# Hybrid decoder layer: block loads moved to another queue, sums and head pairs reordered

## The chip, the cores and the metric

One core of one Trainium2 chip runs the whole layer in one launch. The metric is device time in microseconds, the median of several runs. The kernel before takes 1122.39 us (median of 3 runs, 1122.03 to 1122.48).

## What is computed

One layer on a sequence of 256 tokens with a model width of 2048, all in float32: one input projection, two token mixers side by side (chunked gated linear attention with 4 heads, and differential attention with 16 heads), two branch projections merged by sigmoid gates, an output projection, and a residual sum.

```python
h = rmsnorm(x, pre_norm_g[l])
proj = h @ w_in[l]
(a_q, a_k, a_v, a_g, a_lr, b_q, b_k, b_v, b_g, m_a, m_b) = jnp.split(proj, offsets, axis=-1)
gk = jax.nn.log_sigmoid((a_lr @ gla_gk_w2[l] + gla_gk_b[l]).astype(jnp.float32)) / GATE_LOGIT_NORMALIZER
o_a = gla_chunked(a_q, a_k, a_v, gk)             # reshaped to 4 heads
o_a = rmsnorm(o_a, gla_norm_g[l]).reshape(B, S, GLA_VAL_DIM) * jax.nn.silu(a_g)
y_a = o_a @ w_branch_a[l]
o_b = diff_attention(b_q, b_k, b_v, lam)         # 16 heads, two softmaxes each
o_b = rmsnorm(o_b, diff_norm_g[l]) * (1.0 - lam_init)
o_b = o_b.reshape(B, S, DIFF_VAL_DIM) * jax.nn.silu(b_g)
y_b = o_b @ w_branch_b[l]
merged = jax.nn.sigmoid(m_a) * y_a + jax.nn.sigmoid(m_b) * y_b
x = x + rmsnorm(merged @ w_out[l], post_norm_g[l])
```

## The kernel before, in words

**Products in float32.** Each weight tile is split into a rounded half `hi` (ScalarE, line 244) and a rest `lo` (VectorE, line 245), and TensorE takes three products of the halves of both operands. A weight tile arrives as `raw` (SyncE's queue, line 216) and is split by halves: `emit_half` makes one half ready, up to `AHEAD` = 4 halves before it is used; `raw`, `hi` and `lo` have 3 buffers each. `half_tile` (line 413) uses one half in 12 matmuls of up to 512 columns; `token_major` (line 424) does the 8 halves of 512 output columns; `channel_major` (line 446) does 128 output channels, transposed, in two halves of 8 matmuls of 512 and 8 of 256 columns.

**Four stretches.** First the value columns `v0`, `v2`, `v3` (to about 81 us). Then the *sets* (to about 447 us): five groups of columns computed as 2 x 2 blocks with seven products instead of eight, `PRODUCTS` = (1, 3, 5, 6, 2, 7, 4), each product in four steps (`t`, `h`), 28 steps a set and 140 in all. `phase_steps` (line 77) mixes 64 half tiles of other columns (`others`, line 621) between them. Then the gates of the linear attention (`ag0` to `ag3`), the merge gates and the heads' channel tiles, with both mixers' attention as background tasks. At the end the branch projections `y0` (lines 1035 to 1045) and `y1`, and the output projection.

**A set's blocks.** Four tiles in 4 buffers (`chain`): `a` and `b` for t = 0, 1, loaded whole by `link` (line 171, 1 MB each, SyncE's queue). Products 1 and 5 and 6 and 4 use `a`, products 3 and 7 use `b`, product 2 uses plain tiles `c` (line 189). `follow_set` (line 195) lets GpSimd's queue add a third block to `a` behind product 1 and to `b` behind product 6 (an accumulating transfer of 1 MB, line 201); VectorE adds `b` to `a` ahead of the splits of product 6 (line 192) and `c` to `a` behind those of product 2 (line 199). Products 1, 6, 7 and 4 share one PSUM bank `x`; VectorE reads it between product 7 and product 4 (line 724).

**Background tasks.** `pump(n)` (line 381) lets each of the first n tasks issue its next segment (up to its next `yield`) behind the half tile just issued. `token_major` pumps after every second half tile, `channel_major` is followed by one `pump(2)`. The tasks are `forget_gate` (line 470), `gla_scores` (line 750), `gla_out` (line 838) for both halves of the linear attention's heads, and one `diff_pair` (line 907) for each two heads of the differential attention: fetch of query and key tiles that had been spilled to memory, split into `q2`, `kh`, `kl` (`diff_split`, line 894), and for each head four segments (scores and exponentials; combination; transposes; values, norm and gate), and a last one that transposes and writes `obh`, `obl` (line 984). `settle` (line 1059) finishes every task before the last two half tiles of the first `y1` tile. `token_major` takes two of the four `mm` banks, the tasks use the four `bg` banks.

**Order.** `ag0`-`ag3`, `m01`, heads 0 and 1, `m02`, a loop that pumps until both halves of the linear attention are out (line 1032), `y0`, heads 2 and 3, `m03`, `y1`, output. Group 0's channel tiles are made in the sets' stretch (`EARLY`); for groups 0 to 2 (`STORED`) query and key are spilled, for group 3 they are split at once. For group 3 the values `dv3` and gates `bg3` are made in `diff_heads`.

**Buffers.** Tag `u`: 18 tiles of 4 KB a partition. Tag `u2`: `MORE` = 13 tiles of 4 KB, for the linear attention's temporaries, its result `oah`, `oal` (8 tiles, read by `y0`), `obh`, `obl` (2 for each group, read by `y1`), and group 3's values and gates. Within the tile framework an instruction waits until a buffer of its tile's tag is free; the order of instructions on an engine is the framework's, by the order of the program and its own estimate of what is ready.

Of the kernel before, what the change touches and what calls it, by code (L numbers as in the profile page):

```python
# [14 lines left out]
P = 128  # L15
D = 2048
S = 256
# [12 lines left out]
LEAD = 6  # L30
EARLY = (0,)
STORED = (0, 1, 2)
# [44 lines left out]
def phase_steps():  # L77

    keys = ["v4"] + [f"{name}{hf}{c}" for hf in range(2) for name in ("k", "q") for c in range(4)]
    keys += [f"{name}{g}{c}" for g in EARLY for pair in range(2) for name in ("dq", "dk") for c in (2 * pair, 2 * pair + 1)]  # L80
    keys += ["m00"]
    other = [(key, r, h) for key in keys for r in range(4 if key in ("v4", "m00") else 1) for h in range(2)]
    steps = [("set", s, prod, t, h) for s in range(SETS) for prod in PRODUCTS for t in range(2) for h in range(2)]
    mixed = []
# [7 lines left out]
def hybrid_kernel(ctx: ExitStack, tc, xt, xn, preg, postg, w, w2, gkb, glag, lamv, diffg, ident_d, causal_d, lmask_d, out):  # L92
# [66 lines left out]
    seq += halves_of(*(f"ag{g}" for g in range(4)), "m01") + heads_order(0) + heads_order(1) + halves_of("m02")  # L159
    seq += halves_of(*(f"y0{g}" for g in range(4))) + heads_order(2) + heads_order(3) + halves_of("m03")  # L160
# [10 lines left out]
    def link(s, name, t):  # L171
        count[0] += 1
        c = blocks.tile([P, 2048], F32, tag="chain", name=f"{name}_{count[0]}", bufs=4)
        sp.dma_start(c, weights(f"set{s}", {"a": 0, "b": 6}[name] + t)[0])
        chain[s, name, t] = c

    def emit_set(s, prod, t, h):
        c = slice(1024 * h, 1024 * h + 1024)
        if h == 0 and prod == 1:
            if s == 0:  # L180
                link(s, "a", t)
            link(s, "b", t)
        if h == 0 and prod == 4 and s + 1 < SETS:
            link(s + 1, "a", t)
        n = 4 * PRODUCTS.index(prod) + 2 * t + h + LEAD - 4 * PRODUCTS.index(2)
        if 0 <= n < 4:
            i, j = n // 2, n % 2
            raws[s, i, j] = u([P, 1024], "c")
            sp.dma_start(raws[s, i, j], weights(f"set{s}", 4 + i)[0][:, 1024 * j : 1024 * j + 1024])
        a, b = chain[s, "a", t], chain[s, "b", t]  # L190
        if prod == 6:
            dve.tensor_tensor(out=a[:, c], in0=a[:, c], in1=b[:, c], op=ALU.add)
        return raws[s, t, h] if prod == 2 else (b if prod in (3, 7) else a)[:, c]

    def follow_set(s, prod, t, h):
        c = slice(1024 * h, 1024 * h + 1024)
        a, b = chain[s, "a", t], chain[s, "b", t]
        if prod == 2:
            dve.tensor_tensor(out=a[:, c], in0=a[:, c], in1=raws[s, t, h], op=ALU.add)
        if h == 1 and prod in (1, 6):  # L200
            pool.dma_start(a if prod == 1 else b, weights(f"set{s}", 2 + t)[0], accum_op=ALU.add)

    def emit_plain(j, key, r, h):
# [6 lines left out]
        early = key == "v0"  # L210
        if h == 0:
# [234 lines left out]
    def channel_major(key):  # L446
        o = ps("mm")
        for h in range(2):
            half_channel(o, h, *take(key))
        return o[:, :S], o[:, S:]  # L450
# [19 lines left out]
    def forget_gate():  # L470
# [10 lines left out]
        w2_raw, w2_s = u([P, 1024], "w2_raw"), u([P, 1024], "w2_s", F32R)  # L481
        pool.memset(w2_raw, 0.0)
        for i in range(4):
            pool.dma_start(w2_raw[32 * i : 32 * i + RANK, :], w2)
        yield
# [120 lines left out]
    gspill = [None] * (2 * SETS)  # L606
    ts, heads, m0 = {}, {}, []
# [13 lines left out]
    def others():  # L621
# [24 lines left out]
        for g in EARLY:  # L646
            for pair in range(2):
                for name in ("dq", "dk"):
                    t = t2([P, 2, S], name)
                    for c in range(2):  # L650
                        o = ps("bg")
                        for h in range(2):
# [5 lines left out]
                            yield  # L658
        banks = [ps("bg"), ps("bg")]
# [90 lines left out]
    def gla_scores(hf):  # L750
# [22 lines left out]
        for n, m in enumerate(LEVELS):  # L773
# [10 lines left out]
            if m == 1:  # L784
                pool.tensor_tensor(out=xqv, in0=xqv, in1=view(k, 0, *early), op=ALU.mult)
# [44 lines left out]
        yield  # L830
# [7 lines left out]
    def gla_out(hf, gates):  # L838
# [27 lines left out]
        for j in range(4):  # L866
# [8 lines left out]
            if j % 2:  # L875
# [16 lines left out]
    parts = {}  # L892

    def diff_split(g, pair, tq, tk):
        q2, kh, kl = parts[g, pair] = [u([P, 2, 2, S], name, F32R) for name in ("q2", "kh", "kl")]
        for m in range(2):
            own, other = slice(64 * m, 64 * m + 64), slice(64 - 64 * m, P - 64 * m)
            act.activation(q2[own, m], tq[own], AF.Copy)
            dve.tensor_tensor(out=q2[other, m], in0=tq[own], in1=f32(q2[own, m]), op=ALU.subtract)
            act.activation(kh[own, m], tk[own], AF.Copy)  # L900
            act.activation(kh[other, m], tk[own], AF.Copy)
            dve.tensor_tensor(out=kl[own, m], in0=tk[own], in1=f32(kh[own, m]), op=ALU.subtract)
            pool.memset(f32(kl[other, m]), 0.0)
        done.add(f"split{g}{pair}")
        yield

    def diff_pair(g, pair, values):
# [7 lines left out]
        if g in STORED:  # L915
            tq, tk = (fetch(heads[g, pair, name], name, lambda shape, name, dtype: t2(shape, name)) for name in ("dq", "dk"))
            yield
            yield from diff_split(g, pair, tq, tk)
        while f"split{g}{pair}" not in done:
            yield  # L920
        q2, kh, kl = parts[g, pair]
        vv, uu = values
        for h in (2 * pair, 2 * pair + 1):
# [53 lines left out]
            yield  # L977
# [8 lines left out]
        yield  # L986

    def diff_heads(g):
# [14 lines left out]
        for pair in range(2):  # L1003
            made = []
            for name in () if g in EARLY else ("dq", "dk"):
# [4 lines left out]
                if g in STORED:  # L1010
                    heads[g, pair, name] = spill(t, name)
                else:
                    made.append(t)
            if made:
                tasks.insert(0, diff_split(g, pair, *made))
# [12 lines left out]
    diff_heads(0)  # L1028
    diff_heads(1)
    merge_gate(token_major("m02", 512, x_ops, 2))  # L1030

# [14 lines left out]

    diff_heads(2)
    diff_heads(3)
# [169 lines left out]
```

## Time and profile before

| | before |
|---|---|
| runs, median (lowest to highest) | 1122.39 us (1122.03 to 1122.48) |
| the profiled execution's own time | 1123.6 us |
| its span, first to last instruction | 1121.8 us |
| granted TensorE clock, mean | 0.997 |
| TensorE matmuls busy | 1105.6 us, 5570 matmuls |
| VectorE, ScalarE, GpSimd busy | 831.8, 677.1, 111.8 us |
| memory traffic | 257.76 MB, mean 230 GB/s |

The profile's page gives busy time of each engine and the costliest groups of instructions. In a row of a group the first number behind the bar is its busy time, the second the mean duration of one in ns, the third the idle time of its engine ahead of it. The view of waits has, for each waiting engine and line and each engine that released it, the sum in us, how often, and the longest. PE is TensorE, DVE VectorE, ACT ScalarE, POOL GpSimd, SP SyncE; a `q` behind them means their sequencer. Matmuls overlap: a matmul's duration is longer than the distance to the next one's start.

### The profile page before, as it was taken

To read this page: it belongs to the slowest core of one execution; us is meant where nothing else is said; L and a number is where in the kernel's file an instruction comes from. 1 tells how busy PE (TensorE), PEld (TensorE's weight loads), DVE (VectorE), ACT (ScalarE), POOL (GpSimd) and SP (SyncE) were. 2 spreads that over 40 slices of the span, in tenths; PEclk is the share of its full clock that TensorE was granted. 3 is DMA by queue.
4 is the path that set the end of the run, shared out by engine and by line. 5 is a ranking of instruction groups with operands and counts; after the bars stand their busy time and mean duration, and the time that the engine had idled before them with its cause. 6 is when DMAs were issued, how large, how long until landed. Compare 5 with 4: busy or idle time off the path is not lost. (4 is left out here: it accounts for less than half of the span.)

```text
span 1121.8 us, 15070 instructions
## 1 busy us (share of the span) xinstructions
PE 1105.6 (99%) x5570; PEld 945.4 (84%) x5570; DVE 831.8 (74%) x1160; ACT 677.1 (60%) x997; POOL 111.8 (10%) x165
## 2 busy tenths in 40 slices
PE   9999999999999999999999999999999999999996
PEld 7998888888888888878888888788888888788886
DVE  7878979779789798699965866766676766655463
ACT  7856666666666666765655755655675665444450
POOL 0101010000100100340021202111200010000000
PEclk9999999999999999999999999999999999999998
DMA  8799797696996973945586567565645474556752
GB/s 313 261 412 243 260 321 221 221 304 188 336 254 218 313 210 123 317 167 185 174 291 243 200 220 257 202 228 176 237 165 184 158 308 161 180 188 218 269 188 75
DMA packets 46042, 257.76 MB, mean 230 GB/s; under 512 B 5841, under 2 KB 7377, under 8 KB 23441
## 3 DMA queue, kind: packets, MB, share of 16 engines
q1 hardware_dynamic: 31968, 198.59, 49.4%
q0 software_dynamic: 12992, 56.89, 18.1%
q10 hardware_dynamic: 1008, 1.32, 0.4%
q8 instruction: 43, 0.70, 0.2%
q14 instruction: 31, 0.25, 0.1%
HBM read 236.86 MB, written 19.92 MB: 229 GB/s over the span
## 5 line engine op out<-in xcount | busy, mean ns | idle before, releaser
L245 DVE TENSOR_TENSOR lo<-raw,hi 128x1024 fp32r<-128x1024 f32 (+3 forms) x307 | 369.1, 1205 | 183.8 <-ACT hi L244 180.8
L244 ACT ACTIVATE hi<-raw 128x1024 fp32r<-128x1024 f32 (+3 forms) x307 | 315.8, 1032 | 282.0 <-PE mm L421 144.6
L421 PE MATMUL mm<-hi,xs 128*128 128x512 f32 (+1 forms) x704 | 171.4, 385 | 0.0
L421 PEld LDWEIGHTS mm<-hi,xs 128*128 128x128 f32 x704 | 130.2, 188 | 21.2
L245 DVE TENSOR_TENSOR lo<-a,hi 128x1024 fp32r<-128x1024 f32 x80 | 97.2, 1221 | 19.0 <-ACT hi L244 18.0
L244 ACT ACTIVATE hi<-a 128x1024 fp32r<-128x1024 f32 x80 | 84.7, 1059 | 39.4 <-PE mm L706 20.0
L441 PE MATMUL mm<-xs,hi 128*128 128x512 f32 x384 | 100.5, 396 | 0.0
L441 PE MATMUL bg<-xs,hi 128*128 128x512 f32 x384 | 99.5, 390 | 0.2 <-ACT hi L244 0.2
L421 PE MATMUL mm<-lo,xs 128*128 128x512 f32 (+1 forms) x352 | 91.9, 383 | 0.7 <-DVE lo L245 0.7
L441 PEld LDWEIGHTS bg<-xs,hi 128*128 128x128 f32 x384 | 72.1, 188 | 14.7 <-ACT hi L244 0.6
L441 PEld LDWEIGHTS mm<-xs,hi 128*128 128x128 f32 x384 | 69.2, 189 | 11.8
L421 PEld LDWEIGHTS mm<-lo,xs 128*128 128x128 f32 x352 | 65.8, 188 | 12.9 <-DVE lo L245 1.6
L706 PE MATMUL mm<-hi,xs 128*128 128x512 f32 x240 | 65.1, 393 | 0.8 <-DVE gr L724 0.8
L443 PEld LDWEIGHTS bg<-xs,lo 128*128 128x128 f32 x384 | 52.3, 190 | 4.9 <-DVE lo L245 1.2
L443 PEld LDWEIGHTS mm<-xs,lo 128*128 128x128 f32 x384 | 52.4, 190 | 3.8
L245 DVE TENSOR_TENSOR lo<-b,hi 128x1024 fp32r<-128x1024 f32 x40 | 48.6, 1221 | 8.5 <-ACT hi L244 7.8
L443 PE MATMUL bg<-xs,lo 128*128 128x256 f32 x384 | 53.6, 282 | 0.8 <-DVE lo L245 0.8
L443 PE MATMUL mm<-xs,lo 128*128 128x256 f32 x384 | 53.5, 282 | 0.0
L706 PEld LDWEIGHTS mm<-hi,xs 128*128 128x128 f32 x240 | 44.4, 188 | 9.7 <-DVE gr L724 1.5
L421 PE MATMUL mm<-hi,oah 128*128 128x512 f32 x128 | 50.7, 396 | 0.0
L421 PE MATMUL mm<-hi,obh 128*128 128x512 f32 x128 | 50.7, 399 | 0.0
L421 PE MATMUL mm<-hi,obl 128*128 128x512 f32 x128 | 50.1, 392 | 0.0
(301 smaller groups left out, 1966.6 us busy)
## 6 DMA issues: line engine op xcount, KB each, us to landing
raw<-in_w_dram SPq DMA_DIRECT2D x136, 1024.0 KB, 5.0
raw<-in_w_dram SPq DMA_DIRECT2D x14, 832.0 KB, 6.0
a<-in_w_dram SPq DMA_DIRECT2D x10, 1024.0 KB, 6.3
b<-in_w_dram SPq DMA_DIRECT2D x10, 1024.0 KB, 7.4
c<-in_w_dram SPq DMA_DIRECT2D x20, 512.0 KB, 10.3
a<-in_w_dram POOLq DMA_DIRECT2D x10, 1024.0 KB, 15.1
b<-in_w_dram POOLq DMA_DIRECT2D x10, 1024.0 KB, 9.5
raw<-in_w_dram SPq DMA_DIRECT2D x4, 800.0 KB, 9.7
```

The costliest lines, as they stand in the source:

```text
L244: act.activation(hi_t[:, a:b], r[:, a:b], AF.Copy)
L245: dve.tensor_tensor(out=lo_t[:, a:b], in0=r[:, a:b], in1=f32(hi_t[:, a:b]), op=ALU.subtract)
L421: i = pe.matmul(banks[b][:, :n], a[part][:, P * b : P * b + P], w[:, n * j : n * j + n], start=first, stop=last)
L441: i = pe.matmul(o, hi[:, c], x_pair(kt), start=kt == 0, stop=kt == KT - 1)
L443: i = pe.matmul(o[:, :S], lo[:, c], x_ops(kt)[0], start=False, stop=False)
L706: i = pe.matmul(out, a[part], w[:, 512 * j : 512 * j + 512], start=first, stop=last, skip_group_check=out is x)
```

## The change

The five parts:

1. In the sets, `link` loads go to GpSimd's queue from the second set on and are issued about two steps earlier each (set 0's two `a` blocks with the first half of `v3`); the accumulating transfers go by halves of a tile; the sums `a+b` and `a+c` stand behind the splits of earlier steps.
2. `phase_steps` puts four other half tiles behind the first four steps and spreads the remaining 60 evenly.
3. `gla_scores` multiplies and adds on VectorE what GpSimd did; `w2_raw` is filled during the sets, and `forget_gate` loses its first `yield`.
4. Every pair's query and key are spilled and fetched twice, once on each half of the partitions, so that the split is done on all 128 partitions at once.
5. All heads' channel tiles come ahead of `y0`; a task whose head 0 is done is pumped also at the half tiles between pumps (`pump_eager`); closing `yield`s are dropped; `settle` is called behind the first half tile of `y1`.

```diff
+FRONT = 4
...
-        mixed += other[len(other) * i // len(steps) : len(other) * (i + 1) // len(steps)]
+        due = min(i + 1, FRONT) + (len(other) - FRONT) * (i + 1) // len(steps)
+        mixed += other[put:due]
+        put = due
...
-    seq += halves_of(*(f"ag{g}" for g in range(4)), "m01") + heads_order(0) + heads_order(1) + halves_of("m02")
-    seq += halves_of(*(f"y0{g}" for g in range(4))) + heads_order(2) + heads_order(3) + halves_of("m03")
+    seq += halves_of(*(f"ag{g}" for g in range(4)), "m01") + heads_order(0) + heads_order(1) + heads_order(2)
+    seq += halves_of("m02") + heads_order(3) + halves_of(*(f"y0{g}" for g in range(4)), "m03")
...
-        sp.dma_start(c, weights(f"set{s}", {"a": 0, "b": 6}[name] + t)[0])
+        (pool if s else sp).dma_start(c, weights(f"set{s}", {"a": 0, "b": 6}[name] + t)[0])
...
-        if h == 0 and prod == 1:
-            if s == 0:
-                link(s, "a", t)
-            link(s, "b", t)
-        if h == 0 and prod == 4 and s + 1 < SETS:
-            link(s + 1, "a", t)
+        if h == 0 and s + 1 < SETS and (prod, t) in ((7, 1), (4, 0)):
+            link(s + 1, "a", 1 - t)
+        if h == 0 and s + 1 < SETS and (prod, t) == (4, 1):
+            link(s + 1, "b", 0)
+        if h == 0 and prod == 1 and (s == 0 or t == 0):
+            link(s, "b", t if s == 0 else 1)
...
-        if prod == 6:
-            dve.tensor_tensor(out=a[:, c], in0=a[:, c], in1=b[:, c], op=ALU.add)
...
-        if prod == 2:
-            dve.tensor_tensor(out=a[:, c], in0=a[:, c], in1=raws[s, t, h], op=ALU.add)
-        if h == 1 and prod in (1, 6):
-            pool.dma_start(a if prod == 1 else b, weights(f"set{s}", 2 + t)[0], accum_op=ALU.add)
+        def accumulate(name, i):
+            pool.dma_start(chain[s, name, i][:, c], weights(f"set{s}", 2 + i)[0][:, c], accum_op=ALU.add)
+
+        if prod == 1:
+            accumulate("a", t)
+        i = {(5, 1): 0, (6, 0): 1, (2, 1): 0, (7, 0): 1}.get((prod, t))
+        if i is not None:
+            a = chain[s, "a", i][:, c]
+            second = prod in (5, 6)
+            dve.tensor_tensor(out=a, in0=a, in1=chain[s, "b", i][:, c] if second else raws[s, i, h], op=ALU.add)
+            if second:
+                accumulate("b", i)
...
+    eager = set()
+
+    def advance(some):
+        with tc.issue_after(latest[0]):
+            for task in some:
+                r = next(task, DONE)
+                (eager.add if r == "go" else eager.discard)(task)
+                if r is DONE:
+                    tasks.remove(task)
+
     def pump(n=1):
-        with tc.issue_after(latest[0]):
-            for task in tasks[:n]:
-                if next(task, DONE) is DONE:
-                    tasks.remove(task)
+        advance(tasks[:n])
+
+    def pump_eager():
+        advance([task for task in tasks[:2] if task in eager])
...
-            if q == 6 and settle:
+            if q == 1 and settle:
                 settle()
             half_tile(banks, n, q, ops, *take(key))
             if q % 2 or "gate" not in done:
                 pump(step)
+            else:
+                pump_eager()
...
-            pool.tensor_tensor(out=dst, in0=src[:, :, 0, :], in1=src[:, :, 1, :], op=ALU.add)
-        pool.tensor_tensor(out=suf, in0=q, in1=k, op=ALU.mult)
+            dve.tensor_tensor(out=dst, in0=src[:, :, 0, :], in1=src[:, :, 1, :], op=ALU.add)
+        dve.tensor_tensor(out=suf, in0=q, in1=k, op=ALU.mult)
...
-                pool.tensor_tensor(out=xqv, in0=xqv, in1=view(k, 0, *early), op=ALU.mult)
+                dve.tensor_tensor(out=xqv, in0=xqv, in1=view(k, 0, *early), op=ALU.mult)
...
+    def twice(t, d):
+
+        for h in range(2):
+            rows = slice(64 * h, 64 * h + 64)
+            pool.dma_start(f32(t[rows]), d.rearrange("(m p) i t -> p m i t", m=2))
...
+        raw = u([P, 2, 2, S], "dq")
+        q2, kh, kl = (u([P, 2, 2, S], name, F32R) for name in ("q2", "kh", "kl"))
+        twice(raw, heads[g, pair, "dq"])
+        twice(kl, heads[g, pair, "dk"])
+        yield
+        act.activation(q2, raw, AF.Copy)
+        act.activation(kh, f32(kl), AF.Copy)
+        for m in range(2):
+            other = slice(64 - 64 * m, P - 64 * m)
+            dve.tensor_tensor(out=q2[other, m], in0=raw[other, m], in1=f32(q2[other, m]), op=ALU.subtract)
+        dve.tensor_tensor(out=kl, in0=f32(kl), in1=f32(kh), op=ALU.subtract)
+        yield
...
-            yield
+            yield "go" if h % 2 == 0 else None
...
-    diff_heads(0)
-    diff_heads(1)
+    for g in range(3):
+        diff_heads(g)
     merge_gate(token_major("m02", 512, x_ops, 2))
+    diff_heads(3)
```

More of the change, by code (lines that the diff above doesn't have):

```diff
@@ L30 @@
 LEAD = 6
+FRONT = 4
 EARLY = (0,)
-STORED = (0, 1, 2)
 BIG = 18
@@ L83, in phase_steps @@
     steps = [("set", s, prod, t, h) for s in range(SETS) for prod in PRODUCTS for t in range(2) for h in range(2)]
-    mixed = []
+    mixed, put = [], 0
     for i, step in enumerate(steps):
         mixed.append(step)
-        mixed += other[len(other) * i // len(steps) : len(other) * (i + 1) // len(steps)]
+        due = min(i + 1, FRONT) + (len(other) - FRONT) * (i + 1) // len(steps)
+        mixed += other[put:due]
+        put = due
     return mixed
@@ L210, in emit_plain @@
         early = key == "v0"
+        if key == "v3" and r == 0 and h == 0:
+            for i in range(2):
+                link(0, "a", i)
         if h == 0:
@@ L449, in channel_major @@
             half_channel(o, h, *take(key))
+            if h == 0:
+                pump_eager()
         return o[:, :S], o[:, S:]
@@ L480, in forget_gate @@
             dve.tensor_tensor(out=lrt[r, :], in0=bank[r, :S], in1=f32(top[r, :S]), op=ALU.subtract)
[L481 to L484, printed above, removed]
-        yield
+        w2_s = u([P, 1024], "w2_s", F32R)
         top = u([P, 1024], "w2h", F32R)
@@ L606, in hybrid_kernel @@
     gspill = [None] * (2 * SETS)
+    w2_raw = u([P, 1024], "w2_raw")
     ts, heads, m0 = {}, {}, []
@@ L658, in others @@
                             yield
+        pool.memset(w2_raw, 0.0)
+        for i in range(4):
+            pool.dma_start(w2_raw[32 * i : 32 * i + RANK, :], w2)
         banks = [ps("bg"), ps("bg")]
@@ L829, in gla_scores @@
         done.add(f"scores{hf}")
-        yield
     for hf in range(2):
@@ L874, in gla_out @@
             split_out(bank, hi, lo, glag_s[:, j : j + 1])
-            if j % 2:
+            if j == 1:
                 yield
@@ L890, in hybrid_kernel @@
     obh, obl = [], []
[L892 to L905, printed above, removed]
+    def twice(t, d):
+        for h in range(2):
+            rows = slice(64 * h, 64 * h + 64)
+            pool.dma_start(f32(t[rows]), d.rearrange("(m p) i t -> p m i t", m=2))
     def diff_pair(g, pair, values):
@@ L914, in diff_pair @@
             values.extend(fetch(gspill[2 * g + 4 + i], name, u) for i, name in enumerate(("dv", "ub")))
[L915 to L921, printed above, removed]
+        raw = u([P, 2, 2, S], "dq")
[10 more added lines that the diff above has]
+        yield
         vv, uu = values
@@ L976, in diff_pair @@
                 dve.scalar_tensor_tensor(out=og[:, h % 2, b, :], in0=bank[:, P * b : P * b + P], scalar=e[:, b : b + 1], in1=uu[:, b, hv], op0=ALU.mult, op1=ALU.mult)
-            yield
+            yield "go" if h % 2 == 0 else None
         bank = ps("bg")
@@ L985, in diff_pair @@
         done.add(f"pair{g}{pair}")
-        yield
     def diff_heads(g):
@@ L1009, in diff_heads @@
                     pump(2)
[L1010 to L1015, printed above, removed]
+                heads[g, pair, name] = spill(t, name)
             tasks.append(diff_pair(g, pair, values))
```

4 lines of the change are left out of this document (removed).

## The prediction

> **What bounds the kernel now.** I read the page first, then TensorE's waits, then the stretches, then the moments of the single waits.
>
> ```profile
> span 1121.8 us, 15070 instructions
> PE 1105.6 (99%) x5570; PEld 945.4 (84%) x5570; DVE 831.8 (74%) x1160; ACT 677.1 (60%) x997; POOL 111.8 (10%) x165
> ...
> PE bg L321 <- DVE ones_b L318: 1.6, 1, 1.6
> PE bg L981 <- DVE ogb L976: 1.5, 2, 0.9
> PE bg L443 <- DVE lo L245: 0.8, 1, 0.8
> PE mm L706 <- DVE gr L724: 0.8, 2, 0.5
> PE mm L421 <- DVE lo L245: 0.7, 2, 0.5
> PE bg L404 <- ACT hi L244: 0.7, 1, 0.7
> PE bg L955 <- DVE prob L951: 0.3, 1, 0.3
> PE bg L441 <- ACT hi L244: 0.2, 1, 0.2
> ```
>
> TensorE works 99% of the span, and the change removes no matmul and adds none. So all it can win is in these waits, and the view lists only 6.6 us of them. L321 and L404 (2.3 us) are the start, which the change doesn't touch; 4.3 us in 9 waits are left. A wait costs more than its idle time, because matmuls overlap:
>
> ```profile
> L421 PE MATMUL mm<-hi,xs 128*128 128x512 f32 x576 | 144.5, 392 | 0.0
> ...
> 712.13 16.34 PE mm L421 x72
> ```
>
> The chain has 72 matmuls in 16.34 us, 0.227 us from start to start, while one lasts 0.392 us. At a wait the overlap of 0.165 us is lost too. The 9 waits are worth 4.3 + 9 x 0.165 = **5.8 us**, 0.5% of the span. That is the ceiling; every new wait comes off it. Everything else the change does (it touches the work of VectorE, ScalarE, GpSimd and the transfers) costs nothing unless it makes TensorE wait.
>
> **The change part by part.** *The sets.* The one wait for `lo` at L443 and what VectorE did before it:
>
> ```profile
> 253.46 2.36 DVE L192 TENSOR_TENSOR a<-a,b 128x1024 f32<-128x1024 f32 x2
> 255.74 1.22 DVE L245 TENSOR_TENSOR lo<-raw,hi 128x1024 fp32r<-128x1024 f32 x1
> ...
> 257.01 1.21 PE L443 MATMUL bg<-xs,lo 128*128 128x256 f32 x8 [0.81 <-DVE lo L245]
> ```
>
> Two sums of product 6 run back to back, 2.36 us, ahead of a `lo` that TensorE needs next. In the new code a sum stands behind a split two or more set steps before its result is used, and ScalarE's `hi` no longer waits for it. There are still four sums in four steps, so the density stays; what goes is that they stand in front of the splits. I take this wait as gone: 0.8 + 0.165 = **0.97**.
>
> The two waits for `gr` (VectorE must read bank `x` before product 4 writes it):
>
> ```profile
> 139.87 0.42 DVE L642 TENSOR_TENSOR k<-k,rstd_bc 128x256 f32<-128x256 f32 x1
> 140.20 0.68 DVE L724 TENSOR_TENSOR gr<-mm,p 128x512 f32<-128x512 f32 x1
> ...
> 140.94 1.19 PE L706 MATMUL mm<-hi,xs 128*128 128x512 f32 x4 [0.51 <-DVE gr L724]
> ```
>
> The read stood behind the finish of a key channel, 0.42 us. I counted the mix: of 64 half tiles on 140 steps none is put behind step 23 (the last of product 7) in the first three sets. With 4 in front and 60 on 140, 12 a set, one stands there in every set, and it is the second half of a channel, whose finish then comes after `gr`. Both waits together are 0.8 + 2 x 0.165 = 1.13; since a half tile was there in the trace too (the framework had moved one up), I take two thirds, **0.75**. The wait for `hi` at L441 (0.2) I leave.
>
> The block loads: 16 of 20 move to GpSimd's queue, and 20 accumulating transfers become 40 of half the size. Queue by queue:
>
> ```profile
> a<-in_w_dram SPq DMA_DIRECT2D x10, 1024.0 KB, 6.3
> ...
> a<-in_w_dram POOLq DMA_DIRECT2D x10, 1024.0 KB, 15.1
> ...
> SPq L174 <- DVE lo L245: 42.4, 13, 9.2
> ```
>
> A plain load from GpSimd's queue isn't in this trace; its landing lies between 6.3 us (the same load from SyncE) and 15.1 us (the accumulating one). A load is now issued six set steps ahead of its split: 6 x 6 matmuls x 0.227 = 8.2 us, and three half tiles of 16 matmuls between them add about 8, so 16 us. Even 15.1 fits; I take 0, both ends 0. SyncE stood 42.4 us at these loads with plain tiles queued behind it; but no wait of TensorE's ends at a transfer, so its relief is worth 0 as well. On GpSimd a waiting load now holds back the spills behind it; they give buffers back later, and no wait is for those. Issuing takes GpSimd's time, but it is busy 10% of the span (the page).
>
> On the halves the Trainium skill speaks against the change: "DMA: Bandwidth & Descriptors", section "Bandwidth", wants 1 MiB or more a transfer, and the fit in its section "Anatomy of one DMA" (2.0 us + bytes / 436e3) makes two halves 2 us dearer than one whole, an estimate of 40 us of queue time for 20 tiles. No run here shows a split tile.
> By my count eight steps or more lie between such a transfer and its use, and at 6 x 0.227 us a step that is 10.9 us even without the half tiles between them, 18 with them; 15.1 fits, and two halves side by side move no more bytes. I take 0.
>
> *The linear attention.* The two waits for `lo` at L421 come at 493 and 500 us, in this stretch:
>
> ```profile
> 480.00:520.00 40.00, 39.26 (x182) 32.19 (x181) 38.84 (x43) 23.06 (x30) 13.02 (x10) 1.00 0.47 159
> 520.00:560.00 40.00, 40.00 (x207) 34.10 (x205) 39.28 (x55) 23.82 (x33) 0.00 (x0) 1.00 0.54 184
> ...
> L245 DVE TENSOR_TENSOR lo<-raw,hi 128x1024 fp32r<-128x1024 f32 x62 | 79.7, 1288 | 31.1 <-ACT hi L244 29.4 <-PE bg L473 1.5
> L783 DVE TENSOR_TENSOR xq<-xq,q 128x512 f32<-128x512 f32 x14 | 11.8, 843 | 0.2 <-ACT xq L782 0.2
> L792 DVE TENSOR_TENSOR xk<-xk,k 128x512 f32<-128x512 f32 x12 | 8.3, 689 | 0.0
> L245 DVE TENSOR_TENSOR lo<-a,hi 128x1024 fp32r<-128x1024 f32 x2 | 2.5, 1226 | 0.7 <-ACT hi L244 0.6
> ...
> 490.64 1.95 POOL L785 TENSOR_TENSOR xq<-xq,k 128x512 f32<-128x512 f32 x1 [0.63 <-DVE xq L783]
> ...
> 491.36 2.32 DVE L245 TENSOR_TENSOR lo<-raw,hi 128x1024 fp32r<-128x1024 f32 x1
> ```
>
> VectorE (third busy number) is full for 80 us, so moving GpSimd's work there looks wrong. But the `lo` at 491.36 takes 2.32 us instead of 1.22 while a GpSimd product runs: the two engines slow each other. From the groups, 62 x (1288 - 1226) + 14 x (843 - 689) ns = 6.0 us of VectorE are lost so. The moved work is, for each half of the heads, one pass of 1024, two of 512 and one of 256 columns: 1.22 + 2 x 0.69 + 0.35 = 2.95, so 5.9 us in all. VectorE's load stays as it is, and the stretched `lo` goes. I take half of 0.7 + 2 x 0.165 = 1.03: **0.5**. Against that `forget_gate` without its first `yield` asks for its first product one half tile (12 x 0.227 = 2.7 us) earlier; two ScalarE passes and one VectorE pass must fit. Bounds 0 and 2.7; I take **0.7** lost, nearer 0 since `w2` now lies ready.
>
> *The pairs.* Per pair six ScalarE and four VectorE passes over 64 partitions become two and three; that lightens engines which are not the bound: worth 0. The transfers grow from 6 x 2 to 8 x 4 of 256 KB, and group 3 is spilled too:
>
> ```profile
> dq<-dq POOLq DMA_DIRECT2D x12, 256.0 KB, 3.3
> ...
> L131 POOL DMA_DIRECT2D dq<-dq x6: 536/544/590, 617.2 to 808.0; - x6
> ...
> 640.00:680.00 40.00, 40.00 (x199) 33.78 (x198) 25.20 (x53) 20.78 (x40) 2.62 (x5) 1.00 0.61 215
> ```
>
> Four issues are 4 x 0.54 = 2.2 us of GpSimd, then 3.3 to land: 5.5 us. They stand behind the `rsqrt` of the pair before on GpSimd; from there to the split lie two pumps of two half tiles each, 4 x 2.72 = 10.9 us. Where a group's two value tiles come first (two issues, 1.1 us) it is 6.6. The transfer engines are 61% busy here. I take 0, and keep the other end as a rival.
>
> *The order.* The waits at L981 and L955:
>
> ```profile
> 711.15 0.60 DVE L976 SCALAR_TENSOR_TENSOR ogb<-bg,de,ub 128x128 f32<-128x128 f32 x2
> ...
> 711.55 0.59 PE L981 MATMUL bg<-ident,ogb 128*128 128x128 f32 x2 [0.91 <-DVE ogb L976]
> ...
> 952.79 0.33 PE L955 MATMUL bg<-ident,prob 128*128 128x128 f32 x1 [0.26 <-DVE prob L951]
> ```
>
> The one at 952 and one at 957 are `settle`: by my count of the segments against the pumps, four segments of the last pair are left when it is called. In the new order group 0 starts at `dk13` instead of `m02`, and the last pair ends with `y02`; `settle` finds no task, and `y03` and `m03` run without any. The wait at 711.55 is a last transpose of a pair beside `y0`, whose two tasks go in step; a segment then has as much cover as before, so it may come back elsewhere. All three: 1.5 + 0.3 + 3 x 0.165 = **2.3**. The new segment between pumps brings head 1's transposes nearer to its scores: three half tiles, 8.2 us, instead of four. What must fit is
>
> ```profile
> L938 DVE CUSTOM_DVE_ANT_0 prob<-bg,causal x64: 280/356/425, 654.4 to 948.0; 128x128 f32<-128x128 f32 x32, 128x256 f32<-128x256 f32 x32
> ...
> L944 ACT ACTIVATE prob<-prob,mx,score_scale x64: 477/540/592, 655.8 to 951.2; 128x128 f32<-128x128 f32 x32, 128x256 f32<-128x256 f32 x32
> L944 ACT ACTIVATION_READ_ACCUMULATOR prob<-prob,mx,score_scale x64: 185/187/188, 656.2 to 951.7; 128x1 f32 x64
> ...
> L951 DVE SCALAR_TENSOR_TENSOR prob<-prob,c,prob x32: 350/415/482, 659.5 to 952.6; 128x128 f32<-128x128 f32 x16, 128x256 f32<-128x256 f32 x16
> ```
>
> 4 x 0.356 + 4 x (0.540 + 0.187) + 2 x 0.415 = 5.2 us, with a `lo` of 1.2 and a `hi` of 1.1 in the way 7.5. It fits barely; bounds 0 and 0.7 for each of 8 pairs, I take 0.1 each: **0.8** lost.
>
> **The sum.** 0.97 + 0.75 + 0.5 + 2.3 = 4.5 won, 0.7 + 0.8 = 1.5 lost, 3.0 net. The profiled execution's span becomes 1118.8 and its own time 1123.6 - 3.0 = 1120.6; it ran 1.2 over the median of the runs, so for these 1122.4 - 3.0 = **1119.4 us**. Bounds: all 5.8 won and nothing lost, 1116.6; nothing won but the 2.3 and the upper costs 2.7 + 5.6 lost, 1128.4.
>
> **The rivals.** *Other waits in the same place.* VectorE is full beside the linear attention and dense in the sets; what is taken from one wait may pass to the next `lo`. For it: its load isn't smaller. Against it: the waits are single late instructions, not a lack of throughput. Then 4.5 and 1.5 become about 2 and 2: 1122.4.
>
> *Thirteen `u2` buffers (slower).* When `bg3` ends, `oah` and `oal` hold 8 until `y03`, `obh` and `obl` of groups 0 and 1 hold 4, and group 3's values and gates need 2: fourteen. Before, `y0` came first. If the gates are the ones without a buffer, the two `mm` banks of `bg3` stay taken, and `y0`'s tiles must share the other two: each of `y01`, `y02`, `y03` begins only when the two reads of the tile ahead are through.
>
> ```profile
> L1041 DVE SCALAR_TENSOR_TENSOR part<-part,mm x6: 673/681/689, 677.9 to 731.1; 128x512 f32<-128x512 f32 x6
> ```
>
> 2 x 0.68 behind a `lo` of 1.22 are 2.6 us, three times 7.7: 1119.4 + 7.7 = 1127.1. It decides from the moment a fourteenth tile is asked for before half of `y03`. Against it: the framework may let a pair's last segment wait instead, which costs less, as some 49 us of products without tasks follow.
>
> *The pair fetch comes late (slower).* If the four transfers of a pair run one after the other, their landings add up: 4 x 3.3 = 13.2 us, 2.3 over the 10.9, and with values ahead (1.1 to issue, 3.3 to land) 6.7 over. ScalarE would stand in front of the split, and the ready halves hold two half tiles, 5.4 us. The rest, 1.3 us, TensorE loses at each of the six pairs of groups 0 to 2: 1119.4 + 7.8 = 1127.2. It decides once a fetch takes longer than 10.9 + 5.4 = 16.3 us from that `rsqrt`. Against it: the transfer engines are idle 39% of that stretch. By the Trainium skill, "DMA: Bandwidth & Descriptors", section "Rules for kernel authors", transfers to two partition halves do serialize, since both spread over the same engines. No row of this trace shows two halves of one tile.
>
> **How the numbers follow.** Forecast 0.55; other waits 0.22; buffers 0.15; fetch 0.08. About 0.2% (2.2 us, so 1120.15 and 1124.6) is what a measurement of this kernel can tell from no change. The forecast's own range is 1116.6 to 1121; a tenth of it lies above 1120.15. Faster: 0.5 from the forecast and 0.04 from the first rival, 0.54. Slower: the two slower rivals, 0.23, of which a few hundredths stay below 1124.6, with as many from the first rival. Same: the rest, 0.23. The range, 1116.4 to 1126.0, takes in the first three quarters of what the slower rivals add and leaves out their full price, and with it the sum of all upper costs.
>
> **What would show it.** TensorE's waits should no longer list L981 and L955, nor `lo` at L443, and `gr` once at most; GpSimd should have no products or sums between 460 and 500 us, and `lo` there a mean near 1226 ns. The last pair's L984 should stand ahead of `y03`. It would be wrong if `mm` matmuls of `y0` wait for L1041, if L244 or the pair's split waits for a transfer, if ScalarE's new `hi` of a block waits for its load, or if TensorE waits at L499 of `forget_gate`.

## The result and the profile after

The changed kernel takes **1132.88 us** (median of 4 runs, 1132.66 to 1133.74) against 1122.43 for the kernel before beside it: a ratio of 1.0095, 95% interval 1.0078 to 1.0113. It is slower by 10.7 us, where 3.0 us faster was forecast; the time lies outside the range of 1116.4 to 1126.0.

The page after, then TensorE's waits and the two waits of ScalarE for a pair's fetch (sum in us, how often, the longest; the rows of the start are left out):

```profile
span 1131.9 us, 15103 instructions
PE 1108.0 (98%) x5570; PEld 947.7 (84%) x5570; DVE 825.7 (73%) x1160; ACT 663.7 (59%) x965; POOL 131.1 (12%) x201
```

```profile
PE bg L975 <- DVE prob L971: 6.4, 4, 3.7
PE bg L894 <- DVE ua L887: 2.1, 1, 2.1
...
PE bg L1001 <- DVE ogb L996: 1.5, 3, 0.7
PE mm L442 <- DVE part L1055: 1.3, 2, 0.6
...
PE bg L520 <- issue: 0.4, 1, 0.4
...
ACT kh L936 <- DMA kl<-dk: 9.5, 4, 4.3
ACT q L935 <- DMA dq<-dq: 8.5, 4, 3.7
```

The waits that the change was to remove are gone from the sets and from the linear attention: no `lo`, no `gr`. In the stretches view (PE, PEld, DVE, ACT, POOL busy, granted clock, DMA share, GB/s) the first row of each fence goes from the first matmul of the sets to their last, the second covers the linear attention. In the sets TensorE does the same 1791 matmuls in 361.6 us instead of 365.7 and has no idle time left; GpSimd's 22.71 us beside the linear attention have become 3.46:

```profile
80.75:446.45 365.70, 363.78 (x1791) 308.78 (x1790) 311.22 (x311) 236.66 (x264) 29.14 (x41) 1.00 0.80 248
450.00:560.00 110.00, 109.20 (x523) 90.91 (x521) 96.56 (x113) 71.20 (x94) 22.71 (x21) 1.00 0.60 207
```

```profile
80.45:442.05 361.60, 361.60 (x1791) 309.10 (x1790) 311.27 (x311) 237.43 (x264) 57.20 (x81) 1.00 0.82 252
450.00:560.00 110.00, 109.61 (x528) 92.08 (x527) 96.66 (x126) 69.76 (x90) 3.46 (x5) 1.00 0.57 199
```

(The upper fence is before, the lower after.) New are the stops for `prob` at L975 and for `ua` at L894, 8.5 us together, and the 1.3 us for `part` at L1055, the sign that the prediction named for the `u2` buffers. ScalarE stands 18.0 us at the split of the pairs for `dq` and `dk`.

How a late fetch gets to TensorE is read from the chain of waits, here for the stop at L894 (start, length, what):

```profile
597.01 1.16 POOL kl L920 x2
598.18 5.15 issue
...
603.37 1.08 POOL gssq L346
604.45 1.16 POOL dq L920 x2
...
606.30 0.88 POOL gssq L346
...
607.89 0.62 POOL kl L920
608.52 7.22 DMA kl<-dk
...
615.84 0.04 ACT kh L936
...
620.45 0.75 DVE ua L887
...
621.24 1.33 PE bg L894 x5
```

GpSimd has issued the first pair's fetch by 598.18. Then it stands 5.15 us at a `rsqrt` whose input isn't ready (L346, `gssq` of the linear attention), issues the second pair's query, stands at another `rsqrt`, and only then issues the key, which lands at 615.74. ScalarE stood at the split `kh` for the last 2.84 us of that, and behind it in ScalarE's order lay what `ua` needs. The longest stop, 3.7 us, has the same form: GpSimd's timeline there, with the idle time before an instruction in brackets, and ScalarE's:

```profile
672.31 0.60 POOL L920 DMA_DIRECT2D dq<-dq  x1 [0.23 <-issue]
676.02 2.22 POOL L346 TENSOR_TENSOR de<-de,neg_half 128x2 f32<-128x2 f32 x1 [3.11 <-DVE de L992]
678.20 0.62 POOL L920 DMA_DIRECT2D dq<-dq  x1
```

```profile
682.43 1.06 ACT L935 ACTIVATE q<-dq 128x1024 fp32r<-128x1024 f32 x1 [3.71 <-DMA dq<-dq]
683.40 0.48 ACT L964 ACTIVATE prob<-prob,mx,score_scale 128x128 f32<-128x128 f32 x1
```

The two halves of one tile are issued 5.9 us apart because a `rsqrt` lies between them. ScalarE waits for the second half, and the other pair's exponentials (L964), which need nothing of it, stand behind; TensorE waits for what comes of them.

### The profile page after: what moved, and what is told of

Its sections match the earlier page's. It is cut to its first block, busy times and chain, and to the rows that moved or that the text cites. A ratio compares the mean times of both kernels' runs of the same rounds, so it can differ in the third digit from the quotient of the medians.

```text
span 1131.9 us, 15103 instructions
## 1 busy us (share of the span) xinstructions
PE 1108.0 (98%) x5570; PEld 947.7 (84%) x5570; DVE 825.7 (73%) x1160; ACT 663.7 (59%) x965; POOL 131.1 (12%) x201
## 4 chain that ended last, share of the span: by engine, by line
PE 87%; DMA 4%; DVE 3%; issue 3%; ACT 2%; POOL 1%; DVEq 0%; SPq 0%; POOLq 0%; ACTq 0%
PE mm L442 39%; PE mm L731 17%; PE bg L464 8%; PE mm L464 5%; PE bg L466 4%; PE bg L442 3%; PE mm L466 2%; DMA kl<-dk 2%; PE bg L425 2%; PE mm L410 2%; PE mm L425 2%; DMA dq<-dq 1%; PE bg L834 1%; DVE lo L256 1%; ACT prob L964 0%
## 5 line engine op out<-in xcount | busy, mean ns | idle before, releaser
L256 DVE TENSOR_TENSOR lo<-raw,hi 128x1024 fp32r<-128x1024 f32 (+3 forms) x307 | 365.2, 1192 | 195.6 <-ACT hi L255 188.7
L464 PEld LDWEIGHTS mm<-xs,hi 128*128 128x128 f32 x384 | 70.0, 191 | 11.9
L442 PEld LDWEIGHTS mm<-lo,xs 128*128 128x128 f32 x352 | 66.5, 189 | 11.5
L255 ACT ACTIVATE hi<-b 128x1024 fp32r<-128x1024 f32 x40 | 42.3, 1057 | 14.8 <-PE mm L731 7.4
## 6 DMA issues: line engine op xcount, KB each, us to landing
a<-in_w_dram POOLq DMA_DIRECT2D x20, 512.0 KB, 11.9
```

What stands on the lines that cost most here:

```text
L255: act.activation(hi_t[:, a:b], r[:, a:b], AF.Copy)
L256: dve.tensor_tensor(out=lo_t[:, a:b], in0=r[:, a:b], in1=f32(hi_t[:, a:b]), op=ALU.subtract)
L442: i = pe.matmul(banks[b][:, :n], a[part][:, P * b : P * b + P], w[:, n * j : n * j + n], start=first, stop=last)
L464: i = pe.matmul(o, hi[:, c], x_pair(kt), start=kt == 0, stop=kt == KT - 1)
```

## The experiments

The change was taken apart along its five parts: *sets* (parts 1 and 2), *linear attention* (3), *pairs* (4), *order* (5). The theory after the result: two costs, both named in the prediction as rivals, came together, the pairs' late fetch (its transfers stand in GpSimd's order) and the `u2` buffers. The rivals to it are given with each run. Ratios are to the kernel before, run beside it; the last column is (ratio - 1) x 1122.4 us.

| run | what | us | ratio, 95% interval | against before |
|---|---|---|---|---|
| 1 | after, old pairs | 1125.88 | 1.0027, 1.0014 to 1.0041 | +3.0 |
| 2 | before, new pairs | 1130.77 | 1.0054, 1.0034 to 1.0074 | +6.1 |
| 3 | before, new sets | 1118.73 | 0.9967, 0.9954 to 0.9980 | -3.7 |
| 4 | after, old order | 1126.37 | 1.0025, 1.0013 to 1.0038 | +2.8 |
| 5 | before, new sets and linear attention | 1117.99 | 0.9957, 0.9942 to 0.9972 | -4.8 |
| 6 | as 1, 15 `u2` buffers | 1118.64 | 0.9963, 0.9951 to 0.9976 | -4.2 |
| 7 | as 2, split one segment later | 1132.75 | 1.0088, 1.0067 to 1.0109 | +9.9 |
| 8 | as 2, raw tile in `u2` | 1124.90 | 1.0028, 1.0013 to 1.0044 | +3.1 |
| 9 | after, 15 `u2` buffers | 1128.63 | 1.0049, 1.0032 to 1.0065 | +5.5 |
| 10 | as 9, fetches issued by SyncE | 1117.30 | 0.9947, 0.9932 to 0.9961 | -5.9 |
| 11 | as 2, fetches issued by SyncE | 1126.40 | 1.0035, 1.0022 to 1.0048 | +3.9 |
| 12 | before, group 3 spilled too | 1126.72 | 1.0031, 1.0018 to 1.0044 | +3.5 |
| 13 | after, fetches issued by SyncE | 1121.12 | 0.9987, 0.9977 to 0.9997 | -1.5 |

Executions of one kernel differ by about 5 to 8 us in runs 1, 2, 4, 7, 8, 11 and 12 (run 12: 1124.1 to 1128.9), and by at most 2.5 us in the others; a trace shows one of them.

**Runs 1 to 4: one part undone or done alone.** Run 1, the old `diff_split` and `diff_pair` put back, with all four groups spilled as the new order needs:

```diff
+STORED = (0, 1, 2, 3)
...
-        raw = u([P, 2, 2, S], "dq")
...
-        twice(raw, heads[g, pair, "dq"])
-        twice(kl, heads[g, pair, "dk"])
+            tq, tk = (fetch(heads[g, pair, name], name, lambda shape, name, dtype: t2(shape, name)) for name in ("dq", "dk"))
+            yield
+            yield from diff_split(g, pair, tq, tk)
```

> The changed kernel with the pairs as before: query and key fetched once, split over 64 partitions, for all four groups from the spill; all else as changed. Theory 1 (the doubled fetch of the pairs is the loss: four transfers and four u buffers a pair, which come late, ScalarE stands at the split): TensorE's waits between 640 and 920 us mostly go, 1119 to 1122 us. Theory 2 (the new order is the loss: less cover between a pair's segments, thirteen u2 buffers): it stays at 1129 to 1133 us, with the waits for L1055 and for the pairs' transposes still there.

Run 2, the opposite, only the new pairs in the kernel before (the lines above the other way round):

> The kernel before with the pairs' double fetch and wide split alone. Theory 1: slower, 1128 to 1135 us, ScalarE waiting for the transfers dq and kl. Theory 2: 1121 to 1125 us, because before's order leaves each fetch one pump more.

Run 3, only the sets:

```diff
+FRONT = 4
...
+        due = min(i + 1, FRONT) + (len(other) - FRONT) * (i + 1) // len(steps)
...
+        (pool if s else sp).dma_start(c, weights(f"set{s}", {"a": 0, "b": 6}[name] + t)[0])
...
+            pool.dma_start(chain[s, name, i][:, c], weights(f"set{s}", 2 + i)[0][:, c], accum_op=ALU.add)
```

> The kernel before with the sets' part alone (block loads on GpSimd's queue, halves, sums spread, four half tiles in front). TensorE has no wait left between 100 and 440 us in the changed kernel's trace, where it had about 2.8 us before: both theories say 1119.0 to 1120.5 us.

Run 4, everything but the order (the extra pumping, `settle` and the dropped `yield`s are undone too):

```diff
-    for g in range(3):
-        diff_heads(g)
+    diff_heads(0)
+    diff_heads(1)
     merge_gate(token_major("m02", 512, x_ops, 2))
-    diff_heads(3)
...
+    diff_heads(2)
+    diff_heads(3)
```

> The changed kernel with before's order (y0 ahead of heads 2 and 3, no segments between pumps, closing yields kept, settle late); sets, linear attention and pairs as changed. Theory 1: still slow, 1127 to 1133 us. Theory 2: 1117 to 1121 us.

Measured: the sets alone win 3.7 us, a little more than the 1.9 to 3.4 that were expected. The pairs alone lose 6.1, and ScalarE's waits for them are there without the new order. The changed kernel still loses 3.0 with the old pairs, so the order loses as well; and without the order it loses 2.8. Runs 1 and 4 both lie between the ranges of their two theories: no single part explains the 10.7. In run 2, ScalarE's wait for the key's fetch:

```profile
ACT kh L912 <- DMA kl<-dk: 20.5, 7, 5.2
```

**Runs 5 to 8: the rest of the sum, the buffers, and two ways to relieve the fetch.** Run 5 is run 3 with the linear attention on VectorE, `w2_raw` early and `forget_gate` without its first `yield`:

```diff
-        pool.tensor_tensor(out=suf, in0=q, in1=k, op=ALU.mult)
+        dve.tensor_tensor(out=suf, in0=q, in1=k, op=ALU.mult)
```

> The kernel before with the sets' part and the linear attention's part (products and sums on VectorE, w2 filled early, forget_gate's first yield gone); pairs and order as before. If the linear attention's part keeps what the changed kernel's trace shows (no wait for lo near 490 and 500 us, 1.07 us from start to start; a new wait of 0.4 at forget_gate), 1117.5 to 1118.7 us, a little under the sets alone (1118.7). If VectorE's extra work costs, 1119 to 1121 us. Either way the loss of 10 us isn't here.

Run 6 gives run 1 two more buffers:

```diff
-MORE = 13
+MORE = 15
```

> The changed kernel with before's pairs, as in the first experiment (1125.9 us), and 15 u2 buffers instead of 13. If the fourteenth u2 tile is what the new order costs, the waits for L1066 at y02 and y03 (0.8 us each) go and more with them: 1119 to 1122 us. If the order costs through late pairs, only those 1.6 us go: 1123.5 to 1125 us.

Run 7 puts one more segment between a pair's fetch and its split in run 2:

```diff
         twice(kl, heads[g, pair, "dk"])
         yield
+        yield
         act.activation(q2, raw, AF.Copy)
```

> The kernel before with the new pairs (1126 to 1132 us in the second experiment) and one more segment boundary between the fetch and the split, so that ScalarE reaches the split one pump, 5.4 us, later. If the loss is ScalarE standing in front of transfers that are not there yet (20.5 us at kl in all), most of that wait goes: 1121 to 1124 us. If it is the transfers' or GpSimd's load itself, it stays at 1127 to 1132 us.

Run 8 takes the raw query tile from `u2`, with 15 buffers:

```diff
-        raw = u([P, 2, 2, S], "dq")
+        raw = u2([P, 2, 2, S], "dq")
```

> The kernel before with the new pairs and their raw query tile in a u2 buffer (15 of them), so that a pair takes three u buffers as before. If the fetch is late because it waits for a fourth free u buffer, the transfers are issued earlier and ScalarE waits less: 1121 to 1125 us. If it is late because of four transfers in GpSimd's order, 1126 to 1132 us as before.

Runs 1 and 6 differ only in the buffers: 3.0 + 4.2 = 7.2 us. TensorE's waits of run 6 have none for `part` any more, and its largest beside the start is one for `wt`, which run 1 has too and the kernel before has not:

```profile
PE bg L988 <- ACT wt L982: 1.5, 1, 1.5
```

Run 7 is a miss, and its trace says why. ScalarE's wait for the key fell from 20.5 to 7.5 us, yet TensorE now stops once for 5.9 us. Chain of waits of run 7:

```profile
692.46 1.17 POOL kl L896 x2
693.64 9.10 issue
...
702.78 0.71 POOL de L335
...
703.59 9.41 DMA part<-part
...
713.43 1.07 ACT q L912
```

After its fetches GpSimd stands 9.1 us at a `rsqrt`; a spill of `part` stands behind it, and the split's `q` waits until that spill has landed, since it takes over its buffer. More distance doesn't help while the order of GpSimd stays. Run 8 regained about half of the pairs' loss (+3.1 instead of +6.1), within the range of its buffer theory, but without that theory's sign: ScalarE still waits 18.6 us for the key (20.5 in run 2), and 11.7 for the query (5.5). The intervals of runs 2 and 8 overlap, so this says little.

**Runs 9 to 13: who issues the fetch.** Run 9 is the changed kernel with `MORE = 15`:

> The changed kernel whole, with 15 u2 buffers instead of 13. Theory (the pairs' fetch and the thirteen buffers are two costs that add, about 7 us each): 1132.9 - 7.2 = 1125.7 us; the wait for part at the end goes, that of bg for prob stays. Rival (what the pairs lose at their places swallows the buffers' cost, or the other way round): 1130 or more.

Run 10 changes one word in it, and moves the 32 transfers to SyncE's queue; their number, size, buffers and program order stay:

```diff
-            pool.dma_start(f32(t[rows]), d.rearrange("(m p) i t -> p m i t", m=2))
+            sp.dma_start(f32(t[rows]), d.rearrange("(m p) i t -> p m i t", m=2))
```

> As the kernel above, and the four transfers of a pair are issued by SyncE instead of GpSimd. Theory (the halves of a fetch stand in GpSimd's order behind rsqrt and the other work there): ScalarE's waits for dq and dk fall from 18 us to under 6, the time to 1118.5 to 1121. Rival (it is the length and number of the transfers, or the buffers that they wait for, whoever issues them): 1124 to 1127, and the plain weight tiles behind them on SyncE's queue may come late as well.

Run 11 is the same word in run 2:

> The kernel before with the new pairs alone, the four transfers of a pair issued by SyncE. Theory (GpSimd's order): from 1130.8 down to 1122 to 1124, ScalarE's waits for dk from 20.5 us to under 6. Rival (the transfers' number, or the four u buffers of a pair that are taken earlier and held longer than the old three): 1128 to 1132, with SyncE standing at the fetches and the plain weight tiles behind them.

Run 12 keeps the old pairs and the old order, and only sends group 3's query and key through memory:

```diff
-STORED = (0, 1, 2)
+STORED = (0, 1, 2, 3)
```

> The kernel before with the old pairs, but group 3's query and key are spilled and fetched as well. Theory (the cost is in the fetch onto both halves and its split): 1122.4, no change. Rival (a good part of it is that group 3's two pairs now go through memory): 1124.5 or more, with a wait of ScalarE's for dq or dk late in the kernel.

Run 13 is the same word as in run 10, with 13 buffers:

> The changed kernel with its 13 u2 buffers, and the four transfers of a pair issued by SyncE. Theory (two costs that add, whichever of them is taken away first): 1117.3 + 4.3 to 7.2 = 1121.6 to 1124.5 us, with TensorE's waits for part (mm banks) and in the last pairs back, and none for prob after a late split. Rival (the buffers only cost because the pairs run late; with punctual fetches the fourteenth tile finds a free buffer): 1117 to 1119, without the wait for part.

Run 9 came out between its two theories: the waits for `part` are gone, but only 4.3 us with them. Run 10 lost all stops of TensorE at the pairs and at L894, and beats both kernels (from run 5, 1117.99, it can't be told). Its waits of TensorE without those of the start, and ScalarE's for the fetch:

```profile
PE bg L983 <- ACT wt L977: 0.5, 1, 0.5
PE bg L520 <- issue: 0.4, 1, 0.4
PE bg L953 <- DVE ogb L996: 0.2, 1, 0.2
...
ACT q L935 <- DMA dq<-dq: 4.5, 2, 2.4
ACT kh L936 <- DMA kl<-dk: 4.1, 5, 1.2
```

The 32 fetches from issue to landing, first in the changed kernel, then in run 10:

```profile
DMA to landing us min/median/max: 3.4/5.8/8.8
```

```profile
DMA to landing us min/median/max: 3.6/6.1/8.6
```

A transfer takes no less time than on GpSimd's queue, so length and number were not the cause. That it is GpSimd's order, and not another property of its queue, is read from the chains above; no run keeps the fetches on GpSimd and takes the `rsqrt` out of their way. With run 13 the square is complete, in medians: 13 buffers and GpSimd 1132.9, 15 and GpSimd 1128.6, 13 and SyncE 1121.1, 15 and SyncE 1117.3. The queue is worth 11.8 or 11.3 us, the buffers 4.3 or 3.8: two costs that add, and each is nearly the same whether the other is there or not. Run 13 lies 0.5 us below the range of its theory and 2 us above that of its rival, and its waits refute the rival too:

```profile
PE mm L442 <- DVE part L1055: 1.3, 2, 0.6
PE bg L1001 <- DVE ogb L996: 1.1, 2, 0.7
```

In the old order the queue explains less: run 11 was expected at 1122 to 1124 and still loses 3.9, and so does run 12 (3.5), which has the old split. In both, group 3's pairs, the last to run, fetch what they had at hand before. Run 12's trace has one stop at the place:

```profile
PE bg L933 <- DVE ogb L976: 2.3, 1, 2.3
```

In the chain of waits ahead of it the spill of a key tile takes 4.64 us, its fetch begins only behind that and takes 4.78, and ScalarE stands 2.3 us at the split for it. So run 12 bore out its rival, and its theory of no change was a miss; the prediction has no term for this detour. Run 11 has the detour too, but its trace does not show it as the loss: the stop at that place is 0.8 us (L929), its last matmul starts at 1112.9 us against 1112.2 in the kernel before, and 2.1 of the 2.8 us by which its span is longer lie behind that. What run 11 still loses stays open. With the new order and punctual fetches (run 10) no such stop is left.

## Why the prediction was wrong

**What bounds the kernel.** The best kernel, run 10, wins 5.9 us (4.4 to 7.6 by its interval), and what it has left is the start and 1.1 us in three waits. That this equals the ceiling of 5.8 is luck. From the first matmul of the sets to the last matmul of all, run 10's trace is 1024.2 us long against 1031.4 in the kernel before, 7.2 less, and its sets begin 1.6 us later. The ceiling added up the waits that leave TensorE idle; it has no term for matmuls that start late while the one ahead is still running.

**The sets.** The mechanism was right: no wait for `lo` or `gr` is left. Forecast were 0.97 + 0.75 = 1.72, run 3 has 3.7 (2.2 to 5.2): the term was too small. In the rows above the same matmuls take 365.7 - 361.6 = 4.1 us less, and 4.1 it is in run 3's trace too. All four waits listed there, `hi` at L441 with them, are worth 1.8 + 4 x 0.165 = 2.5. The rest was never idle time: the same 1791 matmuls kept TensorE busy for 363.78 us and now do for 361.60, so some had started late without a gap that the list of waits shows.

**The block loads.** Taken at 0, which runs 3 and 5 bear out. The rows that the prediction had to bound:

```profile
a<-in_w_dram POOLq DMA_DIRECT2D x8, 1024.0 KB, 6.0
b<-in_w_dram POOLq DMA_DIRECT2D x8, 1024.0 KB, 8.6
...
a<-in_w_dram POOLq DMA_DIRECT2D x20, 512.0 KB, 11.9
b<-in_w_dram POOLq DMA_DIRECT2D x20, 512.0 KB, 8.3
```

A plain load on GpSimd's queue lands in 6.0 to 8.6 us, within the bounds of 6.3 and 15.1 but for 0.3; a half accumulating transfer lands in 11.9 and 8.3 instead of 15.1 and 9.5 for a whole one. By the Trainium skill ("DMA: Bandwidth & Descriptors", section "Bandwidth") transfers should be of 1 MiB or more; going below that cost nothing that these runs show.

**The linear attention.** GpSimd's products are gone and the `lo` between 460 and 510 us is no longer stretched (mean in ns behind the busy time; first before, then after):

```profile
L245 DVE TENSOR_TENSOR lo<-raw,hi 128x1024 fp32r<-128x1024 f32 x15 | 22.4, 1498 | 6.2 <-ACT hi L244 6.1
```

```profile
L256 DVE TENSOR_TENSOR lo<-raw,hi 128x1024 fp32r<-128x1024 f32 x18 | 22.0, 1220 | 3.4 <-ACT hi L255 3.4
```

Forecast were 0.5 won and 0.7 lost at `forget_gate`; run 5 against run 3 wins 1.1, less than the intervals tell from nothing. The stop at `forget_gate` came (L520, 0.4 us, not in the list before).

**The order.** The waits of the last pair at L981 and L955 shrink to 0.3 us in run 6, but others come (`wt`, 1.5 us, and `kl`, 0.8): with enough buffers the order loses 4.8 - 4.2 = 0.6 us (run 6 against run 5), where 2.3 - 0.8 = 1.5 won were forecast; the two intervals overlap.

**The pairs: the step that failed.** "Four issues are 4 x 0.54 = 2.2 us of GpSimd, then 3.3 to land: 5.5 us. They stand behind the `rsqrt` of the pair before on GpSimd [...] I take 0." The sum took one `rsqrt` ahead of the four issues, all four in one piece. The trace shows them taken apart: two tasks issue in turn, and ahead of a pair's four transfers and again between them lies a `rsqrt` that waits for another task's `de` or `gssq`. In the chain above it is 11.3 us from a pair's first issue (604.45) to its last landing, and 17.6 from where GpSimd was done with the pair ahead, not 5.5. Run 10 shows that GpSimd as the issuer is the cost: the same transfers from SyncE, 11.3 us less. The rest of the step was right: against the old pairs (run 6, -4.2) the wide split with punctual fetches (run 10, -5.9) costs nothing.

The rival "the pair fetch comes late" had the place (ScalarE in front of the split) and about the size (7.8 against 11.5), but another mechanism: the landings one after the other. The Trainium skill ("DMA: Bandwidth & Descriptors", section "Rules for kernel authors") says that transfers to two partition halves serialize. The transfers are indeed longer than the 3.3 us of before (5.8 in the median), but run 10 has them as long without the loss. The rival stood at 0.08 because 39% idle transfer engines were counted against it; the queue's issuer was never the question asked.

**The buffers.** The rival was priced 7.7 us; 15 buffers instead of 13 are worth 7.2 beside the old pairs and about 4 in the changed kernel. No run has 14, so the count of fourteen tiles stays argued. Its details were off: only two of the three tiles of `y0` wait, 0.6 us each in the list, and a part of the rest lies in the last pairs (L1001), whose wait falls from 1.5 to 0.4 us in run 9, and from 1.1 us in run 13 to nothing in run 10. Why `ogb` came late there is not traced. In run 1's trace, the slowest of its eight executions, the wait for `ogb` in the last pairs is 4.3 us and one stop of it 2.6. The rival got 0.15 because the framework might let something cheaper wait.

**The sum of chances.** Both slower rivals were priced from 1119.4 and treated as if only one could be true. They have different causes and both happened; from the forecast, with both prices, it is 1119.4 + 7.7 + 7.8 = 1134.9, with 1132.9 measured. That this comes so near is partly luck, since one price was too high (7.7 for about 4), the other too low (7.8 for 11.5).

## What to carry to other kernels

A transfer costs its issuer's place in line: before giving one to an engine that also computes, list what that engine may stand at between two issues, with the other tasks' instructions among it, and look whether a queue without arithmetic is free. An in-order engine that converts what was fetched passes a late landing on to every task behind it, so the fetch must be early for the latest of its pieces, not for their median. Count the buffers of a tag at each point of a new order, and add the prices of rivals that don't exclude each other.

## What the hardware did that was not expected

A stop of TensorE can cost more than itself, for behind some stops the granted clock falls. Stretches of 2 us after the stops at 618 us (2.1 us) and 682 us (3.7 us) of the changed kernel; the granted clock is the third number from the end:

```profile
618.00:620.00 2.00, 0.47 (x5) 0.23 (x3) 1.74 (x5) 2.00 (x4) 0.71 (x1) 1.00 0.30 121
620.00:622.00 2.00, 1.30 (x7) 1.07 (x8) 2.00 (x3) 1.03 (x3) 0.00 (x0) 0.76 0.65 152
622.00:624.00 2.00, 2.00 (x7) 1.69 (x6) 2.00 (x5) 1.13 (x2) 0.00 (x0) 0.50 0.89 373
624.00:626.00 2.00, 2.00 (x12) 1.72 (x11) 0.96 (x2) 0.63 (x1) 0.00 (x0) 0.88 0.00 0
...
686.00:688.00 2.00, 1.49 (x5) 1.34 (x6) 1.97 (x5) 2.00 (x5) 0.00 (x0) 0.50 0.28 119
688.00:690.00 2.00, 2.00 (x7) 1.55 (x6) 1.61 (x3) 1.72 (x5) 0.00 (x0) 0.67 0.00 0
...
818.00:820.00 2.00, 0.71 (x5) 0.31 (x4) 1.25 (x5) 2.00 (x7) 0.00 (x0) 1.00 0.95 385
820.00:822.00 2.00, 2.00 (x11) 1.69 (x11) 1.81 (x4) 0.87 (x5) 0.49 (x1) 1.00 0.23 94
```

From the clock, 2 x (0.24 + 0.50 + 0.12) = 1.7 us are lost behind the first stop, on top of it, which is 3.4 us at half rate. Behind the second 2 x (0.50 + 0.33) = 1.7 are an upper end, since TensorE stood until 686.51; the stop in the stretch from 818 us, with 1.3 us idle by its row, leaves the clock at 1.00 behind it. In the kernel before, whose longest stop behind the start is 0.9 us, this never comes up. The Trainium skill ("TensorE: Matmul & The Clock Gate", section "Part 1: The HAM clock gate") has the clock at half after an idle window of about 3.4 us; here a stop of 2.1 us was enough. The length of the stop alone does not decide: one of 1.7 us in run 9 (at L894 too) brought the clock to 0.50, and one of 2.1 us in run 2 (for `ua` too, L870) left it at 1.00. Behind run 12's stop of 2.3 us it stays at 0.50 to 0.75 for 8 us, which costs some 3 us more. A new wait of about 2 us can therefore cost as much again, or more, which the prediction's 0.165 us a wait did not have.
